# Moving the gathers, four weight loads and the selection's evictions across the overflow branch of two mixture-of-experts layers

## The chip, the cores and the metric

The kernel runs on one core of a Trainium2 chip. The metric is the device time of one execution in microseconds (us); less is better. TensorE (PE in the profile, PEld for its weight loads), VectorE (DVE), ScalarE (ACT), GpSimd (POOL) and SyncE (SP) each run their own instruction stream in order and wait for one another through semaphores. SP and POOL, and now and then ACT, also issue DMA transfers.

## The reference

Two transformer layers over 256 latent and 256 context tokens of width 1024. Each layer has a mixer (Fourier and neighbourhood attention in layer 0, retention in layer 1) and then a mixture of 16 experts, of which each token uses two. Only the experts matter here:

```python
def moe_ffn(tok, router_w, router_b, w1, w3, w2):
    scores = jax.nn.sigmoid((tok @ router_w).astype(jnp.float32))
    ...
    for e in range(N_EXPERTS):
        hid = jax.nn.silu(tok @ w1[e]) * (tok @ w3[e])
        out = out + gate[:, e:e + 1] * (hid @ w2[e])
    return out
```

Layer 0 feeds 512 tokens to the experts, layer 1 the 256 latent ones.

## The kernel before

Every weight matrix of an expert comes as two tiles of 1 MB (`raw`, 128 partitions by 2048 floats), six tiles for an expert: two each of `moe_w1`, `moe_w3` and `moe_w2`. `split` turns a tile into four halves' worth of operands: ScalarE rounds each half to `whi` (L176), VectorE subtracts to get `wlo` (L178), and TensorE makes three products for every weight block (`mm3`, L317 to L319): `whi` with `xh`, `wlo` with `xh`, `whi` with `xl`. `raw` tiles rotate through six slots, `whi`/`wlo` pairs through a small ring of their own, so loads wait until a slot has been split and splits until a pair has been multiplied.

The rows of one expert are brought together first. In **layer 0** (`moe`, `expert`) the router gives each expert up to 128 tokens, in a list `tok`. `e_gather(e)` (L1018) is an indirect DMA on GpSimd's queue that fetches expert e's rows of `xd` into `xg[e % 2]`; `e_tr(e)` transposes them on TensorE (`tsp`, L670) and splits them into `xh`, `xl`. The hidden value `g` (L1064, L1065) is transposed (`tsp`, L670) and split into `gh`, `gl` and multiplied by `moe_w2` into `y_ps`. In **layer 1** (`moe1`, `expert1`) the router gives each group of four experts up to 128 tokens. Group 0's rows are not gathered: `select_group0` multiplies the tokens with a selection matrix on TensorE (`sel_ps`, L1432), and its evictions write `xh` (ScalarE, L1436) and `xl` (VectorE, L1437). Groups 1 to 3 are gathered.

Where more than 128 tokens fall to an expert or a group, extra passes are needed. They stand in a branch over all engines (`overflow`, L1101, and `overflow1`, L1553): every engine loads the flag `R["ovf"]` into a register (L690, L1451) and jumps over the body when it is zero, which is the case in the runs here. `branch_hint` places a prefetch hint on each engine ahead of it. On GpSimd the path around the body waits for the DMAs that GpSimd has issued and then adds to their semaphores what the body would have added (INC_SWDGE_SEM).

The Tile scheduler orders each engine's stream: among what is ready in its own plan it takes what was traced first. So work traced behind the branch can be issued ahead of it, if it doesn't depend on the branch's body. `issue_after(ins)` adds an edge of order alone: what the block traces on the engine of `ins` is queued behind `ins`.

Before the change, layer 0 traces the register load (L690), sets up the experts (`experts_setup`, which also writes zeros into `xg`, L1028), traces the branch, and behind it the gather for expert 0, two tiles of `moe_w3` and two of `moe_w2` of expert 0 loaded from GpSimd's queue (L157 with `self.ld = nc.gpsimd`), the gather for expert 1, the transposes of expert 0, and the gather for expert 2. All other weight tiles are loaded from SP's queue. Layer 1 traces the selection, products and evictions, ahead of its branch, with the products in PSUM bank set `psp`.

Of the kernel before, what the change touches and what calls it, by code (L numbers as in the profile page):

```python
# [7 lines left out]
F32 = mybir.dt.float32  # L8
# [3 lines left out]
AF = mybir.ActivationFunctionType  # L12
ALU = mybir.AluOpType
# [92 lines left out]
def weight_block(A, name, layer, e, k, n):  # L106
    key = ((layer, e), 0, 4, 512 * n, 512) if name == "moe_w2" else ((layer, e), k - k % 4, 4, 0, 512)
    return A[name][TILE_AT[name][key], :, 512 * (k % 4):512 * (k % 4) + 512]


class Net:
# [564 lines left out]
    def moe(self, layer, NT):  # L676
        nc = self.nc
        assert layer == 0
        with ExitStack() as es:
            rp = self.pool(es, f"moe_r{layer}", 1)  # L680
            psp = self.pool(es, f"moe_tp{layer}", 3, space=PSUM)
            hps = self.pool(es, f"moe_h{layer}", 3, space=PSUM)
            yps = self.pool(es, f"moe_y{layer}", 2, space=PSUM)
            fin = [self.ada_mm(1, c, (hps, "h"), psp) for c in self.fill]
            self.prefetch([("moe_w1", (0, 0), 4 * i, 4, 0, 512) for i in range(2)])
            R = self.route(layer, NT, rp, psp)
            with self.tc.issue_after(R["dve"].ins):
                for f in fin:
                    f()
            rv = nc.values_load(R["ovf"][0:1, 0:1], min_val=0, max_val=1)  # L690
            self.branch_hint(layer, R)
            self.g2 = [self.mod_bc(rp, layer, G2, i, tag=f"g2{i}") for i in range(NT // 2)]
            ep = self.pool(es, f"moe_e{layer}", 2)
            self.xs = [[ep.tile([128, 8, 128], F32R, name=f"{n}{i}", bufs=1) for n in ("xh", "xl")] for i in range(2)]
            self.facc = ep.tile([128, 2, D], F32, name="facc", bufs=1)
            last = R["dve"]
            after = lambda: (es2.enter_context(self.tc.issue_after(i.ins)) for i in (last, self.rt_act))
            with ExitStack() as es2:
                list(after())
                xg = self.experts_setup(layer, NT, R, ep, psp, hps, yps)  # L700
            self.overflow(rv, self.facc[:, 0], self.facc[:, 1])
            with ExitStack() as es2:
                list(after())
                es2.enter_context(self.tc.issue_after(self.zeroed.ins))
                first = self.e_gather(0)
                es2.enter_context(self.tc.issue_after(first.ins))
                self.ld = nc.gpsimd
                self.prefetch([("moe_w3", (0, 0), 4 * i, 4, 0, 512) for i in range(2)])
                self.prefetch([("moe_w2", (0, 0), 0, 4, 512 * n, 512) for n in range(2)])
                self.ld = nc.sync  # L710
                self.e_gather(1)
                self.e_tr(0)
                self.e_gather(len(xg))
                self.e_hid(0, "moe_w1", 0)
                R["weights"]()
                self.expert(0)
            for e in range(1, 16):
                self.expert(e)
            self.hx.close()
            self.moe0_tail(ep, psp, hps)  # L720
# [699 lines left out]
        nc.vector.tensor_tensor(gw, gw, tb[:, 16:32], ALU.add)  # L1420
        return nc.vector.tensor_tensor(gw, gw, tb[:, 32:48], ALU.add)

    def select_group0(self, NT, R, P, psp):
        nc = self.nc
        xh, xl = self.xs[0]
        for t in range(NT):
            nc.vector.tensor_scalar(P[:, t], self.cb[:, 2], 1.0, R["rs0"][:, t:t + 1], ALU.add, ALU.is_equal)
        for b0 in (0, 4):
            tp = psp.tile([128, 512], F32, tag="tp", name="sel_ps")
            for b in range(4):  # L1430
                for t in range(NT):
                    nc.tensor.matmul(tp[:, 128 * b:128 * b + 128],  # L1432
                                     self.xm[t][:, 128 * (b0 + b):128 * (b0 + b) + 128], P[:, t],
                                     start=(t == 0), stop=(t == NT - 1))
            tv = tp.rearrange("p (b q) -> p b q", q=128)
            nc.scalar.activation(xh[:, b0:b0 + 4], tv, AF.Copy)  # L1436
            nc.vector.tensor_tensor(xl[:, b0:b0 + 4], tv, xh[:, b0:b0 + 4].bitcast(F32), ALU.subtract)  # L1437

    def moe1(self):
        nc = self.nc  # L1440
        NT = 2
        with ExitStack() as es:
            rp = self.pool(es, "moe_r1", 1)
            psp = self.pool(es, "moe_tp1", 3, space=PSUM)
            hps = self.pool(es, "moe_h1", 3, space=PSUM)
            fin = [self.ada_mm(1, c, (hps, "h"), psp) for c in self.fill]
            R = self.route1(NT, rp, psp)
            with self.tc.issue_after(R["dve"].ins):
                for f in fin:
                    f()  # L1450
            rv = nc.values_load(R["ovf"][0:1, 0:1], min_val=0, max_val=1)  # L1451
            self.branch_hint(1, R)
            self.fg = rp.tile([128, D], F32, name="fng")
            nc.gpsimd.dma_start(self.fg, self.A["final_norm_g"].partition_broadcast(128))
            self.g2 = [self.mod_bc(rp, 1, G2, 0, tag="g20")]
            yps = self.pool(es, "moe_y1", 1, space=PSUM)
            ep = self.pool(es, "moe_e1", 2)
            self.xs = [[ep.tile([128, 8, 128], F32R, name=f"{n}{i}", bufs=1) for n in ("xh", "xl")] for i in range(2)]
            scr = ep.tile([128, 2, D], F32, name="scr", bufs=1)
            hg = [ep.tile([128, D], F32, name=f"hg{i}", bufs=1) for i in range(4)]  # L1460
            last = R["dve"]
            after = lambda: (es2.enter_context(self.tc.issue_after(i.ins)) for i in (last, self.rt_act))
            self.select_group0(NT, R, scr[:, 0, 0:128 * NT].rearrange("p (t s) -> p t s", s=128), psp)
            xg = self.xg
            self.X = X = dict(layer=1, NT=NT, T=128 * NT, R=R, ep=ep, psp=psp, hps=hps, yps=yps, xg=xg, xs=self.xs,
                              hs={}, per=4, hg=hg, ss=ep.tile([128, 4, 2], F32, name="oss", bufs=1))
            with ExitStack() as es2:
                list(after())
                nc.gpsimd.memset(xg[0], 0.0)
            self.overflow1(rv, scr)  # L1470
            with ExitStack() as es2:
                list(after())
                for g in range(1, 4):
                    self.gather(xg[g - 1], self.xd, R["tok"][:, g:g + 1], 256)
                self.e_hid(0, "moe_w1", 0)
                R["weights"]()
                self.expert1(0)
            for g in range(4):
                nc.gpsimd.memset(hg[g], 0.0)
                self.gather(hg[g], self.hd, R["tok"][:, g:g + 1], 256)  # L1480
            for e in range(1, 16):
                self.expert1(e)
            self.hx.close()
# [63 lines left out]
    def overflow1(self, rv, scr):  # L1547
        nc, A, tc, X = self.nc, self.A, self.tc, self.X
        V = nc.vector
        NT, R, ep, psp, xg, hg = (X[k] for k in ("NT", "R", "ep", "psp", "xg", "hg"))  # L1550
        x, ya, gT, hr = xg[0], xg[1], xg[2][:, 0:512].rearrange("p (b q) -> p b q", q=128), hg[0]
        xT = scr[:, 1].rearrange("p (b q) -> p b q", q=128)
        with tc.If(rv > 0, label="ovf1"):  # L1553
# [15 lines left out]
            def product(lhs, nk, w):  # L1569
                ps = psp.tile([128, 512], F32, tag="tp", name="f_ps")  # L1570
                for k in range(nk):
                    nc.gpsimd.dma_start(fw, w(k))
                    nc.tensor.matmul(ps, lhs[:, k], fw, start=(k == 0), stop=(k == nk - 1))
                return ps

            for g in range(4):
# [6 lines left out]
                for e in range(4 * g, 4 * g + 4):  # L1583
                    nc.scalar.activation(fg, product(xT, 8, lambda k: weight_block(A, "moe_w1", 1, e, k, 0)),
                                         AF.Silu)
                    ps = product(xT, 8, lambda k: weight_block(A, "moe_w3", 1, e, k, 0))
                    V.scalar_tensor_tensor(fg, ps, gw[:, e:e + 1], fg, ALU.mult, ALU.mult)
                    transposed(gT, fg, 4)
                    for n in range(2):
                        ns = slice(512 * n, 512 * n + 512)  # L1590
                        ps = product(gT, 4, lambda k: weight_block(A, "moe_w2", 1, e, k, n))
# [6 lines left out]
                V.scalar_tensor_tensor(hr, hr, r, self.fg, ALU.mult, ALU.mult)  # L1598
                self.scatter_out(hr, tok[:, g:g + 1])
            self.slots1(NT, R, 0, psp, tok, tokf)  # L1600

    def dump(self, name, view):
        if name in self.dbg:
            self.nc.sync.dma_start(self.dbg[name], view)
# [49 lines left out]
```

## Time and profile before

| | us |
|---|---|
| three timed runs | 1297.39, 1297.54, 1301.25 |
| median of them | 1297.54 |
| the profiled execution's own time | 1300.92 |
| its span, first to last instruction | 1299.1 |

| engine | busy us, share of the span |
|---|---|
| TensorE matmuls | 1208.8, 93% |
| TensorE weight loads | 945.9, 73% |
| VectorE | 941.4, 72% |
| ScalarE | 752.8, 58% |
| GpSimd | 125.9, 10% |

The mean granted clock of TensorE is 0.973 of full speed (1.00 is 2.4 GHz, 0.50 is 1.2 GHz). The experts of layer 0 stand at 330 to 640 us of the span, those of layer 1 at 983 to 1283 us. In a row of a timeline the columns are start, duration, engine, line, operation, written tile, shapes, count of merged instructions, and in brackets how long the engine sat idle before it and what ended that. A letter q behind an engine marks its sequencer.

### The profile page before, as it was taken

Reading aid. Unit: us, or ns where it says so; the run is one execution under the profiler, and the core shown is the slowest. Engines: PE = TensorE matmul, PEld = TensorE weight load, DVE = VectorE, ACT = ScalarE, POOL = GpSimd, SP = SyncE. Lnnn points to the kernel's source line nnn. Section 1 sums busy time; section 2 is a strip of 40 time slices with the busy share of each in tenths; the row PEclk is TensorE's granted clock in tenths of the full one; section 3 lists DMA queues with packets and bytes.
Section 4 is the critical chain, followed back from the end, with each engine's and each line's share of the span. In section 5 each row is a group of like instructions: output and inputs, shape, how many; then the busy total and the mean of one; then the engine's idle time right before and its main releaser. Section 6 shows DMA issues by size and latency. Waiting matters only on the chain. (4 is left out here: it accounts for less than half of the span.)

```text
span 1299.1 us, 18749 instructions
## 1 busy us (share of the span) xinstructions
PE 1208.8 (93%) x7081; PEld 945.9 (73%) x7081; DVE 941.4 (72%) x1593; ACT 752.8 (58%) x1118; POOL 125.9 (10%) x126
## 2 busy tenths in 40 slices
PE   5999999898599999999989999999997999999994
PEld 3777666576488877777667888898776788777673
DVE  4755666856598888888897554454657899888984
ACT  3754565723397778778554333343434787677762
POOL 1010002200211112111000000000003000000020
PEclk8999999999799999999989999999998999999997
DMA  9766673342799999999883445422749899899980
GB/s 344 259 239 253 250 269 141 124 160 82 311 349 373 358 357 359 362 368 349 305 318 113 149 158 202 153 107 97 289 167 391 339 353 376 317 346 349 327 312 9
DMA packets 60885, 340.60 MB, mean 262 GB/s; under 512 B 10252, under 2 KB 14860, under 8 KB 24144
## 3 DMA queue, kind: packets, MB, share of 16 engines
q1 hardware_dynamic: 46656, 303.07, 61.8%
q0 software_dynamic: 11392, 31.81, 7.5%
q10 hardware_dynamic: 2736, 4.41, 1.0%
q8 instruction: 59, 0.97, 0.3%
q14 instruction: 42, 0.34, 0.1%
HBM read 333.74 MB, written 18.40 MB: 271 GB/s over the span
## 5 line engine op out<-in xcount | busy, mean ns | idle before, releaser
L178 DVE TENSOR_TENSOR wlo<-raw,whi 128x1024 fp32r<-128x1024 f32 x471 | 557.6, 1219 | 115.2 <-ACT whi L176 113.8
L176 ACT ACTIVATE whi<-raw 128x1024 fp32r<-128x1024 f32 x476 | 478.3, 1052 | 95.2 <-PE qk_ps L318 24.7
L318 PE MATMUL h_ps<-wlo,xh 128*128 128x512 f32 x512 | 208.9, 408 | 8.2 <-DVE wlo L178 8.0
L317 PE MATMUL h_ps<-whi,xh 128*128 128x512 f32 x512 | 204.3, 400 | 0.0
L319 PE MATMUL h_ps<-whi,xl 128*128 128x512 f32 x512 | 203.9, 398 | 0.1
L318 PEld LDWEIGHTS h_ps<-wlo,xh 128*128 128x128 f32 x512 | 96.8, 189 | 47.2 <-DVE wlo L178 28.3
L317 PEld LDWEIGHTS h_ps<-whi,xh 128*128 128x128 f32 x512 | 96.9, 189 | 21.7 <-ACT whi L176 0.4
L319 PEld LDWEIGHTS h_ps<-whi,xl 128*128 128x128 f32 x512 | 96.8, 189 | 19.5 <-issue 0.5
L274 PE MATMUL ada_ps<-raw,cT 128*32 128x128 f32 x1536 | 54.6, 279 | 0.6 <-DMA raw<-in_ada_w 0.6
L317 PE MATMUL y<-whi,gh 128*128 128x512 f32 x128 | 51.4, 401 | 0.9 <-ACT gh L673 0.9
L318 PE MATMUL y<-wlo,gh 128*128 128x512 f32 x128 | 51.5, 402 | 0.6 <-DVE wlo L178 0.6
L317 PE MATMUL y_ps<-whi,gh 128*128 128x512 f32 x128 | 51.4, 401 | 0.7 <-ACT gh L673 0.7
L318 PE MATMUL y_ps<-wlo,gh 128*128 128x512 f32 x128 | 51.7, 404 | 0.0
L319 PE MATMUL y<-whi,gl 128*128 128x512 f32 x128 | 51.1, 408 | 0.5 <-DVE gl L674 0.4
L319 PE MATMUL y_ps<-whi,gl 128*128 128x512 f32 x128 | 51.2, 405 | 0.1
L274 PEld LDWEIGHTS ada_ps<-raw,cT 128*32 128x32 f32 x1536 | 42.1, 111 | 12.5 <-issue 8.8
L673 ACT ACTIVATE gh<-tsp 128x512 fp32r<-128x512 f32 x32 | 19.1, 597 | 46.8 <-PE tsp L670 46.7
L673 ACT ACTIVATE xh<-tsp 128x512 fp32r<-128x512 f32 x38 | 22.3, 596 | 31.9 <-PE tsp L670 31.9
L317 PE MATMUL qk_ps<-xhi,whi 128*128 128x512 f32 x96 | 39.4, 411 | 0.0
L1092 POOL DMA_INDIRECT moe_sum<-y,tok x15 | 26.2, 1748 | 133.4 <-ACT y L1087 133.4
L318 PE MATMUL qk_ps<-xlo,whi 128*128 128x512 f32 x96 | 38.8, 404 | 0.0
L1018 POOL DMA_INDIRECT xg<-xd,tok x19 | 25.8, 1356 | 130.8 <-PE tsp L670 109.5
(437 smaller groups left out, 2401.1 us busy)
## 6 DMA issues: line engine op xcount, KB each, us to landing
raw<-in_moe_w SPq DMA_DIRECT2D x188, 1024.0 KB, 7.7
raw<-in_ada_w SPq DMA_DIRECT2D x48, 1024.0 KB, 6.6
raw<-in_ret_w_in SPq DMA_DIRECT2D x24, 1024.0 KB, 6.5
raw<-in_mixab_w_in SPq DMA_DIRECT2D x10, 1024.0 KB, 6.4
raw<-in_ret_w_out SPq DMA_DIRECT2D x8, 1024.0 KB, 4.9
raw<-in_mixab_w_out SPq DMA_DIRECT2D x4, 1024.0 KB, 7.0
raw<-in_moe_w POOLq DMA_DIRECT2D x4, 1024.0 KB, 7.9
bias<-in_rpb ACTq DMA_DIRECT2D x12, 256.0 KB, 5.3
```

The lines of the kernel that those rows point to most:

```text
L176: self.nc.scalar.activation(hi, r, AF.Copy)
L178: eng.tensor_tensor(lo, r, hi.bitcast(F32), ALU.subtract)
L274: mm = nc.tensor.matmul(ps[32 * j:32 * j + 32, 0:128], self.cT[:, kk, :], raw[:, k, 128 * j:128 * j + 128], start=(kk == 0), stop=(kk == 7 ...
L317: mm(out, lh, rh, start=first, stop=False)
L318: mm(out, lh, rl, start=False, stop=False)
L319: self.mm_last = mm(out, ll, rh, start=False, stop=last)
L673: nc.scalar.activation(hi[:, b0:b0 + w], tv, AF.Copy)
L1018: return self.nc.gpsimd.indirect_dma_start(out=x, out_offset=None, in_=xd[:, :], in_offset=bass.IndirectOffsetOnAxis(ap=idx, axis=0), boun ...
L1092: nc.gpsimd.indirect_dma_start(out=self.F[:, :], out_offset=bass.IndirectOffsetOnAxis(ap=R["tok"][:, e:e + 1], axis=0), in_=y, in_offset=N ...
```

## The change

In layer 0 the gather for expert 0, the four weight loads from GpSimd's queue and the gather for expert 1 are traced ahead of the branch, in that order, and the register load is queued behind the second gather on GpSimd. The gather for expert 2 stays behind the branch. In layer 1 the selection is cut in two: the products are traced ahead of the branch, now in the bank set `hps`, and the evictions (`split_group0`) behind it. A write to `xh` and `xl` at the end of the branch's body makes the evictions depend on the branch, so that they can't be issued ahead of it.

```diff
-            rv = nc.values_load(R["ovf"][0:1, 0:1], min_val=0, max_val=1)
             self.branch_hint(layer, R)
...
                 xg = self.experts_setup(layer, NT, R, ep, psp, hps, yps)
+                first = self.e_gather(0)
+            with self.tc.issue_after(first.ins):
+                self.ld = nc.gpsimd
+                self.prefetch([("moe_w3", (0, 0), 4 * i, 4, 0, 512) for i in range(2)])
+                self.prefetch([("moe_w2", (0, 0), 0, 4, 512 * n, 512) for n in range(2)])
+                self.ld = nc.sync
+                second = self.e_gather(1)
+            with self.tc.issue_after(second.ins):
+                rv = nc.values_load(R["ovf"][0:1, 0:1], min_val=0, max_val=1)
             self.overflow(rv, self.facc[:, 0], self.facc[:, 1])
             with ExitStack() as es2:
                 list(after())
                 es2.enter_context(self.tc.issue_after(self.zeroed.ins))
-                first = self.e_gather(0)
-                es2.enter_context(self.tc.issue_after(first.ins))
-                self.ld = nc.gpsimd
-                self.prefetch([("moe_w3", (0, 0), 4 * i, 4, 0, 512) for i in range(2)])
-                self.prefetch([("moe_w2", (0, 0), 0, 4, 512 * n, 512) for n in range(2)])
-                self.ld = nc.sync
-                self.e_gather(1)
                 self.e_tr(0)
                 self.e_gather(len(xg))
...
-    def select_group0(self, NT, R, P, psp):
+    def select_group0(self, NT, R, P, ps):
...
-            tp = psp.tile([128, 512], F32, tag="tp", name="sel_ps")
+            tp = ps.tile([128, 512], F32, tag="h", name="sel_ps")
...
+            tps.append(tp)
+        return tps
+
+    def split_group0(self, tps):
+        nc = self.nc
+        xh, xl = self.xs[0]
+        for i, tp in enumerate(tps):
             tv = tp.rearrange("p (b q) -> p b q", q=128)
-            nc.scalar.activation(xh[:, b0:b0 + 4], tv, AF.Copy)
-            nc.vector.tensor_tensor(xl[:, b0:b0 + 4], tv, xh[:, b0:b0 + 4].bitcast(F32), ALU.subtract)
+            b = slice(4 * i, 4 * i + 4)
+            nc.scalar.activation(xh[:, b], tv, AF.Copy)
+            nc.vector.tensor_tensor(xl[:, b], tv, xh[:, b].bitcast(F32), ALU.subtract)
...
             self.overflow1(rv, scr)
             with ExitStack() as es2:
                 list(after())
+                self.split_group0(tps)
                 for g in range(1, 4):
...
             self.slots1(NT, R, 0, psp, tok, tokf)
+            for w in self.xs[0]:
+                V.memset(w.bitcast(F32)[:, 0:8:4, 0:1], 0.0)
```

## Rows read from the trace of the kernel before

**Rows 1.** Windows in layer 0: length, busy of each engine, PEclk, DMA share, GB/s

```profile
325.00:330.00 5.00, 0.20 (x1) 0.00 (x0) 2.62 (x7) 0.00 (x0) 2.27 (x2) 0.50 0.60 186
...
340.00:345.00 5.00, 4.35 (x19) 3.23 (x18) 2.69 (x5) 3.89 (x4) 0.00 (x0) 1.00 1.02 431
...
350.00:355.00 5.00, 1.72 (x8) 1.75 (x9) 0.00 (x0) 0.60 (x1) 0.00 (x0) 0.50 1.02 417
...
400.00:420.00 20.00, 20.00 (x96) 16.07 (x95) 17.41 (x18) 16.35 (x21) 3.01 (x2) 1.00 0.99 376
```

**Rows 2.** Timeline of TensorE in layer 0, around the gather for expert 1

```profile
353.28 1.94 PE L670 MATMUL tsp<-cst,xg 128*128 128x128 f32 x8 [7.30 <-DMA xg<-xd,tok]
355.01 1.06 PE L670 MATMUL tsp<-cst,g 128*128 128x128 f32 x4
356.46 0.66 PE L670 MATMUL tsp<-cst,xg 128*128 128x128 f32 x2 [0.39 <-DMA xg<-xd,tok]
356.77 0.78 PE L317 MATMUL y_ps<-whi,gh 128*128 128x512 f32 x1
```

**Rows 3.** Timeline of GpSimd's issues in layer 0: gathers and weight loads

```profile
325.02 1.68 POOL L1018 DMA_INDIRECT xg<-xd,tok  x1 [8.39 <-DVE adab L282]
326.70 0.60 POOL L157 DMA_DIRECT2D raw<-in_moe_w  x1
334.99 1.65 POOL L157 DMA_DIRECT2D raw<-in_moe_w  x3 [7.70 <-PE h_ps L319]
336.95 1.41 POOL L1018 DMA_INDIRECT xg<-xd,tok  x1 [0.30 <-issue]
```

**Rows 4.** Line 1101, layer 0's branch: duration ns min/median/max, first and last start

```profile
L1101 POOLq EVENT_SEMAPHORE  x5: 17/43/43, 329.5 to 333.3; - x5
...
L1101 PEldq COMPARE_BRANCH  x1: 3722/3722/3722, 325.4 to 325.4; - x1
...
L1101 DVEq COMPARE_BRANCH  x1: 84/84/84, 325.9 to 325.9; - x1
...
L1101 DVEq EVENT_SEMAPHORE  x1: 21/21/21, 329.3 to 329.3; - x1
L1101 POOLq INC_SWDGE_SEM  x1: 931/931/931, 333.4 to 333.4; - x1
```

**Rows 5.** Issue to landing: the load at 326.70, gathers at 338.67 and 372.68

```profile
DMA to landing us min/median/max: 6.4/6.4/6.4
...
DMA to landing us min/median/max: 17.7/17.7/17.7
...
DMA to landing us min/median/max: 9.8/9.8/9.8
```

**Rows 6.** Timeline of layer 0: VectorE's product g, SP's first loads

```profile
348.48 0.68 DVE L1065 TENSOR_TENSOR g<-g,h_ps 128x512 f32<-128x512 f32 x1
...
337.45 7.21 SPq L157 DMA_DIRECT2D raw<-in_moe_w  x4
```

**Rows 7.** Timeline of layer 1 from the selection to TensorE's longest wait

```profile
971.07 5.77 ACT L176 ACTIVATE whi<-raw 128x1024 fp32r<-128x1024 f32 x6
...
978.70 2.35 DVE L178 TENSOR_TENSOR wlo<-raw,whi 128x1024 fp32r<-128x1024 f32 x2
...
983.51 0.48 PE L317 MATMUL h_ps<-whi,xh 128*128 128x512 f32 x1
...
984.42 0.69 DVE L1437 TENSOR_TENSOR xl<-sel_ps,xh 128x512 fp32r<-128x512 f32 x1 [0.99 <-ACT xh L1436]
...
985.03 4.62 DVE L178 TENSOR_TENSOR wlo<-raw,whi 128x1024 fp32r<-128x1024 f32 x4
...
992.86 0.19 DVE L1375 TENSOR_TENSOR of<-oa,og 128x32 f32<-128x32 f32 x1 [3.21 <-DVEq L1553]
...
1003.15 0.56 PE L318 MATMUL h_ps<-wlo,xh 128*128 128x512 f32 x1 [4.34 <-DVE wlo L178]
```

**Rows 8.** Line 1553, layer 1's branch, on VectorE's sequencer

```profile
L1553 DVEq COMPARE_BRANCH  x1: 74/74/74, 986.9 to 986.9; - x1
```

More of the change, by code (lines that the diff above doesn't have):

```diff
@@ L1421, in slot_weights1 @@
         return nc.vector.tensor_tensor(gw, gw, tb[:, 32:48], ALU.add)
-    def select_group0(self, NT, R, P, psp):
+    def select_group0(self, NT, R, P, ps):
         nc = self.nc
-        xh, xl = self.xs[0]
+        tps = []
         for t in range(NT):
@@ L1462, in moe1 @@
             after = lambda: (es2.enter_context(self.tc.issue_after(i.ins)) for i in (last, self.rt_act))
-            self.select_group0(NT, R, scr[:, 0, 0:128 * NT].rearrange("p (t s) -> p t s", s=128), psp)
+            tps = self.select_group0(NT, R, scr[:, 0, 0:128 * NT].rearrange("p (t s) -> p t s", s=128), hps)
             xg = self.xg
```

## The prediction

> **What bounds the kernel now.** I read the windows first. In the middle of layer 0's experts TensorE is busy for all of a stretch of 20 us, at the full clock of 2.4 GHz [rows 1]; so there the time is TensorE's work, and only what happens ahead of such a stretch can be won or lost, one for one. Next I looked for the holes at the start of each expert stage. The timeline of TensorE in layer 0 has one of 7.30 us, ended by the landing of expert 1's gather, and a small one of 0.39 us for expert 2's gather [rows 2]. Behind the hole the clock stands at 0.50, which is 1.2 GHz, while in the window ahead of it it was 1.00 [rows 1].
>
> Why does that gather land so late? GpSimd issued expert 0's gather at 325.02 and one weight load at 326.70, and then nothing until 334.99 [rows 3]. The releaser printed there is TensorE, but the rows of the branch tell more: GpSimd's sequencer goes through the semaphores of its DMAs until 333.3 and then through the 0.93 us of INC_SWDGE_SEM [rows 4]. The load of 326.70 lands 6.4 us later, at 333.1 [rows 5], just ahead of that. So GpSimd's way around the branch ends only once what GpSimd has issued has landed, and from landing to the next issue it takes 334.99 - 333.1 = 1.9 us. Three loads and the gathers for experts 1 and 2 stand behind it. Meanwhile the DMA engines ran at a share of 0.60 and 186 GB/s; later, with SP's loads added from 337.45 [rows 6], at 431 GB/s, which is full [rows 1]. The gather is late because it was queued late and then had to share.
>
> In layer 1 the hole is on TensorE at 1003.15, 4.34 us, ended by a weight split on VectorE; VectorE itself lost 3.21 us at 992.86 to its own branch [rows 7].
>
> **Layer 0, step by step.** The change takes three loads and expert 1's gather from behind GpSimd's branch and puts them ahead. Issue: three loads take 1.65 us in all [rows 3], so they would go out from 327.3 to 329.0 and the gather at about 329.2, 7.7 us earlier than 336.95. They need `raw` slots that layer 1's two modulation chunks leave; the load at 326.70 took one of the same four slots without a wait.
>
> Landing: the first load should land at 333.1 as before. Each further MB (1.05e6 bytes) takes 1.05/0.431 = 2.4 us at the full rate, three take 7.3 us, and the gather's 0.52e6 bytes 1.2 us: 341.6 with nothing beside them. SP's loads start at 337.45 and share the tail; if the last 2.2 us of work go at half rate it is 343.8. At half rate from the start it would be 333.1 + 17 = 350. I take 344, near the first, because SP's slots still have to be split before it can load.
>
> What is late next: TensorE's last product ahead of the hole ends at 353.28 - 7.30 = 345.98 [rows 2], so a gather at 344 costs nothing. Then comes `g`. VectorE made it at 348.48 (0.68 us) [rows 6], behind splits of a `moe_w2` tile that had only just landed; with that tile landing some 8 us earlier these splits can come first. From the transposes of `g` to the first `y_ps` it takes 356.77 - 355.01 = 1.76 us [rows 2]. So `y_ps` starts between 345.98 + 0.68 + 1.76 = 348.4 and 348.48 + 0.68 + 1.76 = 350.9, against 356.77: 8.3 to 5.9 us are won. More is possible, since the low clock after the hole goes with it (the eight transposes at 353.28 took 1.94 us at 1.2 GHz; at 2.4 GHz half of that is an estimate of 1.0 won). Less is possible, since VectorE's splits all crowd forward. I take -6.5 us, with -9 and -3 as ends.
>
> What waits for the added order: behind GpSimd's branch stands expert 2's gather, and behind that expert 0's scatter, which isn't needed before 360. GpSimd's branch itself costs nothing to others as long as that gather is in time (the rivals). The branch may also come later on the other engines, because the scheduler now has more time to place work ahead of it. TensorE's branch took 3.72 us, 325.4 to 329.1, and VectorE's 3.4 us, 325.9 to 329.3 [rows 4], both under the wait for expert 0's gather (issued at 325.02; at the 6.4 us of the load behind it, it lands about 331). If one of them comes behind the first transposes, that cover is gone and it costs between 0 and 3.7 us; most of that VectorE and TensorE have in hand before 345.98, since they wait for loads. I take 0, inside the ends above. SP and ScalarE leave their branch at once, nothing there.
>
> **Layer 1, step by step.** No work is added; the two evictions on ScalarE and the two on VectorE now stand behind the branch, and every product on `h_ps` needs them. The bank set `hps` has three banks, two of which the modulation chunks hold until VectorE has added their bias, ahead of its split at 978.70, so the products aren't held for long. ScalarE is idle and its branch is short. VectorE decides. It can split only the six halves that ScalarE has rounded (x6 at 971.07); at 4.62/4 = 1.16 us each from 978.70 it is done at 985.6 [rows 7]. Before, its branch was taken at 986.9 [rows 8] with work queued to 985.03 + 4.62 = 989.65, so the sequencer runs 2.7 us ahead; now it would branch at 982.9. From branch to next instruction it was 992.86 - 986.9 = 6.0 us here [rows 7, 8], and 3.4 us in layer 0 [rows 4]. So the first `xl` (0.69 us) is there between 982.9 + 3.4 + 0.7 = 987.0 and 982.9 + 6.0 + 0.7 = 989.6. TensorE starts `h_ps` at 983.51 now [rows 7]; it would start in earnest 3.5 to 6.1 us later. Against that VectorE has no gap at 992.86 any more (3.21 us), and TensorE no hole of 4.34 us at 1003.15 [rows 7], for VectorE does the same splits either way. The two cancel to -0.8 to +1.8 us; the low clock that followed one hole may follow the other. I take 0, with -3.5 and +3 as ends, for VectorE's later small waits may go too.
>
> [...]
>
> **The sum.** -6.5 + 0 = -6.5 us. The profiled execution took 1300.92 us (span 1299.1), so it would take 1294.4; that execution is 3.4 us above the median of the timed runs, 1297.54, and the same difference from the median gives 1291.
>
> **The rivals.** *A, the forecast*: both holes of layer 0 go; 1291 (1287 to 1294). For it: the loads have free slots and idle DMA engines; 0.45.
>
> *B, the hole moves to expert 2's gather.* TensorE takes its stream in order, and that stream has expert 2's transposes right behind those of `g`, ahead of most of `y_ps` [rows 2]. Now that gather can't be issued until all that GpSimd issued has landed: 344 + 1.9 = 345.9. With 6.4 us to landing (the nearest uncontended row) it is there at 352.3, with 9.8 us at 355.7 [rows 5]. If the scheduler leaves those transposes where they are, TensorE waits there instead of at 353.28 and wins only 356.46 - 352.3 = 4.2 to 0.8 us, 2.5 as a middle: 1295. Against it: the scheduler orders by its own plan, and with weights there earlier it has other products to place first; 0.22.
>
> *C, the same place, slower.* The gather for expert 2 took 17.7 us to land when SP's loads filled the engines [rows 5]. If expert 1's gather lands at 348 and this one takes 9.8 to 17.7 us, it is there at 348 + 1.9 + 9.8 = 359.7 to 367.6, and TensorE stands until then: 3 to 11 us worse than 356.46, 1302 with 4.5. It decides from the moment that this landing falls behind 356.46, and only if the transposes keep their place; 0.15. [...]
>
> *D, layer 1 loses.* VectorE's splits ahead of the branch and the fetch add up, and the clock falls in the new hole: +3 us, so 1294 with A's gain; 0.10.
>
> *E, nothing of it shows*: the loads are issued early but `y_ps` waits for VectorE's splits all the same: 1297; 0.08.
>
> **How the numbers follow.** About 0.3% (3.9 us) is what a measurement of this kernel can tell from no change. Faster by more: nearly all of A, a third of B, some of D: 0.43 + 0.07 + 0.04 = 0.54. Slower by more: most of C and a little elsewhere: 0.14. Within: 0.32. For 8 in 10 the range leaves out the best tenth of A, where the clock's gain and layer 1's -3.5 us come together below 1285, and the worse half of C above 1300: 1285 to 1300.
>
> **What would show it.** Right: GpSimd's four loads and two gathers in a row from 325 to 331; expert 1's gather landed by 346; no wait above 1 us at TensorE's second set of transposes; the first `y_ps` near 350 and the clock at 1.00 through 345 to 360. In layer 1: VectorE's wait behind its branch ahead of the first `xl`, TensorE's first `h_ps` at 987 to 990, and no hole near 1003. Wrong: a wait for expert 2's gather at 347 to 360 (B, C), a branch on TensorE or VectorE in the midst of the first products, or a new hole above 6 us behind the selection's products (D).

## The result, and the profile after it

| | before | changed kernel |
|---|---|---|
| median of the timed runs, side by side, us | 1298.60 | 1290.39 |
| lowest and highest of them, us | 1295.5, 1301.74 | 1287.46, 1293.8 |
| ratio, 95% interval | | 0.993 (0.9915 to 0.9946) |
| the profiled execution's own time, us | 1300.92 | 1289.99 |
| its span, us | 1299.1 | 1288.2 |

The change makes the kernel 0.7% faster, 8.2 us between the medians. The forecast was 6.5 us, all of it from layer 0. The size is near; the place is not. Run alone, layer 0's part is worth nothing that can be measured, and layer 1's part is worth 7.4 us.

In the profile after it the line numbers of layer 0 have moved by 1 (L1102 is the branch, L1019 the gather), those of layer 1 by 1 to 10 (L1433 is the selection's product, L1446 the eviction `xl`, L1563 the branch).

**Layer 0.** GpSimd's issues, in a timeline of the changed kernel (start, duration, engine, line, operation, tile, count, idle time before and what ended it), answer to [rows 3]:

```profile
324.61 1.68 POOL L1019 DMA_INDIRECT xg<-xd,tok  x1 [8.40 <-DVE adab L282]
326.30 2.15 POOL L157 DMA_DIRECT2D raw<-in_moe_w  x4
328.75 1.05 POOL L1019 DMA_INDIRECT xg<-xd,tok  x1 [0.30 <-issue]
347.46 1.01 POOL L1019 DMA_INDIRECT xg<-xd,tok  x1 [17.65 <-PE h_ps L319]
```

The issue from gather 1 to its landing, which answers to [rows 5]:

```profile
DMA to landing us min/median/max: 16.8/16.8/16.8
```

Four loads and two gathers go out in a row, and gather 1, issued at 328.75, lands at 345.5. That much is as forecast. Now TensorE's timeline of the same stretch, which answers to [rows 2]:

```profile
336.22 1.94 PE L670 MATMUL tsp<-cst,xg 128*128 128x128 f32 x8 [11.43 <-DVEq L1102]
337.99 0.79 PE L317 MATMUL h_ps<-whi,xh 128*128 128x512 f32 x1
...
348.38 1.03 PE L670 MATMUL tsp<-cst,xg 128*128 128x128 f32 x8
...
353.52 0.50 PE L317 MATMUL h_ps<-whi,xh 128*128 128x512 f32 x1 [1.31 <-ACT xh L673]
...
355.28 0.80 PE L319 MATMUL h_ps<-whi,xl 128*128 128x512 f32 x1 [1.02 <-DVE xl L674]
...
359.86 0.43 PE L317 MATMUL y_ps<-whi,gh 128*128 128x512 f32 x1
```

The transposes of expert 1 (348.38) start without a wait: the hole of 7.30 us is gone. But the first transposes, of expert 0, start at 336.22 behind 11.43 us of idle time, which VectorE's branch ended; before, they started at 330.56 behind 5.36 us, as two lines of the kernel before show that [rows 2] doesn't have:

```profile
330.56 1.94 PE L670 MATMUL tsp<-cst,xg 128*128 128x128 f32 x8 [5.36 <-DMA xg<-xd,tok]
...
343.14 0.50 PE L318 MATMUL h_ps<-wlo,xh 128*128 128x512 f32 x1 [0.65 <-DVE wlo L178]
```

Add up the holes of the stretch: before, 5.36 + 0.65 + 7.30 + 0.39 = 13.70 us; now 11.43 + 1.31 + 1.02 = 13.76 us. The hole moved, and its sum stayed.

Why VectorE's branch is late shows in the timelines of ScalarE (first line) and VectorE, and in the rows of the branch:

```profile
332.46 2.00 ACT L176 ACTIVATE whi<-raw 128x1024 fp32r<-128x1024 f32 x2 [11.01 <-DMA raw<-in_moe_w]
```

```profile
328.81 1.03 DVE L785 TENSOR_SCALAR S<-cb,tokf 128x128 fp32r<-128x128 bf16 x4
333.55 2.36 DVE L178 TENSOR_TENSOR wlo<-raw,whi 128x1024 fp32r<-128x1024 f32 x2 [3.72 <-ACT whi L176]
336.06 0.36 DVE L965 TENSOR_TENSOR t<-of,sc 128x64 f32<-128x64 f32 x2
```

```profile
L1102 DVEq COMPARE_BRANCH  x1: 84/84/84, 335.1 to 335.1; - x1
L1102 DVEq EVENT_SEMAPHORE  x1: 21/21/21, 335.9 to 335.9; - x1
```

Ahead of the branch now stand two splits (333.55) that were not there before. They are those of expert 0's first `moe_w3` tile, the load that GpSimd issues at 326.30 and that lands at 332.4. With that load ahead of the branch, the scheduler had its splits to place ahead of the branch too. VectorE waits 3.72 us for them, takes its branch at 335.1 instead of 325.9 [rows 4], and TensorE's transposes wait for VectorE behind that branch. The way around the branch isn't the cost: from branch to next step it is 0.8 us here, at 335.95, and VectorE was in its split until 335.91.

**Layer 1.** The timelines of TensorE, VectorE and ScalarE and the branch's rows of the changed kernel answer to [rows 7, 8]:

```profile
974.72 3.62 PE L1433 MATMUL sel_ps<-scr,xg 128*128 128x128 f32 x30
983.36 0.80 PE L317 MATMUL h_ps<-whi,xh 128*128 128x512 f32 x1 [5.03 <-issue]
```

```profile
975.65 6.89 DVE L178 TENSOR_TENSOR wlo<-raw,whi 128x1024 fp32r<-128x1024 f32 x6
982.70 0.19 DVE L1376 TENSOR_TENSOR of<-oa,og 128x32 f32<-128x32 f32 x1 [0.16 <-DVEq L1563]
...
983.39 1.28 DVE L1446 TENSOR_TENSOR xl<-sel_ps,xh 128x512 fp32r<-128x512 f32 x2
```

```profile
982.71 1.08 ACT L1445 ACTIVATE xh<-sel_ps 128x512 fp32r<-128x512 f32 x2 [8.42 <-DVEq L1563]
```

```profile
L1563 DVEq COMPARE_BRANCH  x1: 74/74/74, 976.1 to 976.1; - x1
...
L1563 DVEq EVENT_SEMAPHORE  x1: 21/21/21, 982.6 to 982.6; - x1
```

VectorE does its six splits in one go from 975.65 to 982.54. Its sequencer had handed all six to the engine and taken the branch by 976.1, so whatever the branch costs passes under them: 0.16 us of idle time are left of the 3.21 us in [rows 7]. TensorE pays a hole of 5.03 us ahead of the first `h_ps`, and there is no hole behind it up to 1013. The write that ties the evictions to the branch is VectorE's, for `xh` as for `xl`; so ScalarE's `xh` waits 8.42 us for VectorE's branch, and the first `h_ps` with it.

For both layers it helps to count TensorE's products. Each layer's experts make 1152 products of 128x512 (lines 317 to 319), so the start of the n-th says how far the work is. The tables give those starts in us as the trace has them, for layer 0 from the start of gather 0, for layer 1 from the start of the last modulation product (L274); the kernels beside before and after are those of the next section.

| layer 0 | 1st | 37th | 73rd | 289th | 1152nd |
|---|---|---|---|---|---|
| before | 7.3 | 17.1 | 38.6 | 93.0 | 316.7 |
| changed kernel | 13.4 | 24.6 | 37.9 | 92.3 | 313.7 |
| layer 0 alone | 13.6 | 24.7 | 37.9 | 92.3 | 313.8 |
| splits deferred | 8.5 | 29.8 | 39.8 | 94.2 | 315.7 |
| deferred, gather 1 first | 7.6 | 23.1 | 34.5 | 88.9 | 310.8 |
| deferred, gather 1 in the middle | 7.3 | 18.5 | 34.3 | 88.7 | 310.2 |
| gather 1 in the middle, not deferred | 13.2 | 24.0 | 38.8 | 93.2 | 314.7 |

| layer 1 | 1st | 37th | 73rd | 145th | 1152nd |
|---|---|---|---|---|---|
| before | 10.1 | 18.9 | 34.1 | 53.4 | 309.4 |
| layer 0 alone | 7.2 | 16.1 | 31.9 | 51.3 | 307.9 |
| evictions free again | 7.2 | 16.1 | 32.0 | 51.3 | 305.8 |
| changed kernel | 12.5 | 22.5 | 31.4 | 48.6 | 301.0 |
| layer 1 alone | 12.8 | 22.8 | 31.7 | 48.8 | 301.3 |
| splits behind the branch | 11.1 | 23.9 | 34.4 | 52.1 | 305.9 |

### The profile page after: what moved, and what is told of

Read it like the earlier page. It is cut to its first block, busy times and chain, and to the rows that moved or that the text cites. A ratio compares the mean times of both kernels' runs of the same rounds, so it can differ in the third digit from the quotient of the medians.

```text
span 1288.2 us, 18793 instructions
## 1 busy us (share of the span) xinstructions
PE 1197.9 (93%) x7081; PEld 943.8 (73%) x7081; DVE 943.1 (73%) x1593; ACT 755.2 (59%) x1118; POOL 126.1 (10%) x126
## 5 line engine op out<-in xcount | busy, mean ns | idle before, releaser
L274 PE MATMUL ada_ps<-raw,cT 128*32 128x128 f32 x1536 | 53.6, 275 | 1.6 <-DMA raw<-in_ada_w 1.5
L317 PE MATMUL y_ps<-whi,gh 128*128 128x512 f32 x128 | 51.3, 401 | 0.7 <-ACT gh L673 0.7
L274 PEld LDWEIGHTS ada_ps<-raw,cT 128*32 128x32 f32 x1536 | 41.3, 109 | 13.2 <-issue 8.7
L318 PE MATMUL qk_ps<-xlo,whi 128*128 128x512 f32 x96 | 38.8, 404 | 0.0
L319 PE MATMUL qk_ps<-xhi,wlo 128*128 128x512 f32 x96 | 38.4, 400 | 0.0
L1554 POOL DMA_INDIRECT out_dram<-hg,tok x4 | 11.0, 2740 | 260.2 <-DVE hg L1548 209.4
```

The lines of the kernel that those rows point to most:

```text
L274: mm = nc.tensor.matmul(ps[32 * j:32 * j + 32, 0:128], self.cT[:, kk, :], raw[:, k, 128 * j:128 * j + 128], start=(kk == 0), stop=(kk == 7 ...
L317: mm(out, lh, rh, start=first, stop=False)
L318: mm(out, lh, rl, start=False, stop=False)
L319: self.mm_last = mm(out, ll, rh, start=False, stop=last)
L1554: self.nc.gpsimd.indirect_dma_start(out=self.out[:, :], out_offset=bass.IndirectOffsetOnAxis(ap=idx, axis=0), in_=x, in_offset=None, bound ...
```

## The experiments

Theory 1 is the prediction: the gain is layer 0's, -6.5 us, and layer 1 gives nothing. Theory 2 is read from the trace above: layer 0's hole only moved, and layer 1 gains because VectorE's branch lies under work that is already queued.

**One layer at a time.** The first kernel has the diff in `moe` alone, the second the rest of it (`select_group0`, `split_group0`, `moe1`, `overflow1`).

> Layer 0's part of the change, with layer 1 as before. Theory 1 (the prediction): expert 1's gather lands by 346, its hole of 7.30 us goes, the whole gain is here: -6.5 us, a ratio of 0.995 (0.993 to 0.998). Theory 2 (read from the trace of the changed kernel): the hole only moves. TensorE's first transposes start at 336.2 instead of 330.6, since VectorE's branch now stands behind the split of a moe_w3 tile that lands at 332.4; so what is won at 353 is lost at 330, layer 0 is worth 0 to -3 us, a ratio of 0.998 to 1.000.

Measured: ratio 0.9997 (0.9985 to 1.0009), that is -0.4 us (-2.0 to +1.2).

> Layer 1's part of the change, with layer 0 as before. Theory 1 (the prediction): 0 us (-3.5 to +3), a ratio of 0.997 to 1.002. Theory 2 (from the trace of the changed kernel): VectorE now takes its branch at the start of its six splits, not behind them, so the code fetch passes under work that is queued already, and TensorE's hole near 1003 goes; layer 1 is worth -5 to -8 us, a ratio of 0.994 to 0.996.

Measured: 0.9943 (0.9924 to 0.9962), -7.4 us (-9.9 to -4.9). By the intervals theory 2 fits both, theory 1 neither. No trace shows what VectorE's branch waits for, a fetch of code or anything else. The trace of layer 0 alone has the same holes as the changed kernel:

```profile
336.93 1.94 PE L670 MATMUL tsp<-cst,xg 128*128 128x128 f32 x8 [11.62 <-DVEq L1102]
...
354.04 0.50 PE L317 MATMUL h_ps<-whi,xh 128*128 128x512 f32 x1 [1.17 <-ACT xh L673]
...
355.79 0.80 PE L319 MATMUL h_ps<-whi,xl 128*128 128x512 f32 x1 [1.02 <-DVE xl L674]
```

**Is it the `moe_w3` split that holds the branch?** In this kernel ScalarE and VectorE may not take the splits of expert 0's `moe_w3` before they have evicted its transposes, which stand behind the branch. `transpose_split` returns its last two instructions, and:

```diff
-                self.e_tr(0)
+                self.tr0 = self.e_tr(0)
...
-        self.e_hid(e, "moe_w3", 0)
+        with ExitStack() as q:
+            for i in self.tr0 if e == 0 else ():
+                q.enter_context(self.tc.issue_after(i.ins))
+            self.e_hid(e, "moe_w3", 0)
```

> The changed kernel, with the splits of expert 0's moe_w3 tiles queued behind the evictions of its transposes on ScalarE and VectorE, so that they cannot stand ahead of the branch there. Theory 2: the first transposes start at 330 to 333 instead of 336.2, and TensorE then meets expert 1's gather (landing at 345.5) or the moe_w3 splits earlier than it has them: of the 3.2 to 6.2 us some 3 remain, 3 us below the changed kernel, a ratio to the kernel before of 0.990 to 0.992. Rival: the landing of the moe_w3 tiles binds anyway, and the two kernels are the same, 0.993.

Measured: 0.9924 (0.9904 to 0.9945). TensorE's timeline, and gather 1's landing, in this kernel:

```profile
333.55 1.94 PE L670 MATMUL tsp<-cst,xg 128*128 128x128 f32 x8 [6.54 <-DVE wk L971]
...
355.01 1.94 PE L670 MATMUL tsp<-cst,xg 128*128 128x128 f32 x8 [9.29 <-DMA xg<-xd,tok]
```

```profile
DMA to landing us min/median/max: 23.9/23.9/23.9
```

The step itself is shown: VectorE's branch is taken at 328.4, and the first transposes start 333.55 - 326.83 = 6.7 us behind gather 0's issue instead of 11.6. Gather 0 lands at 333.4 in this kernel, so next to nothing of that start is VectorE's any more. But the time isn't measurably below the changed kernel's; it lies as near to the rival's 0.993 as to theory 2's range, for a reason that neither named. The hole at gather 1 is back, and longer than before the change: 9.29 us. Gather 1 was issued at 330.97 and needed 23.9 us. The cause is on SP's queue, in its timelines of the changed kernel (first line) and of this one (second):

```profile
335.94 1.41 SPq L157 DMA_DIRECT2D raw<-in_moe_w  x3
```

```profile
328.86 13.37 SPq L157 DMA_DIRECT2D raw<-in_moe_w  x3
```

SP's loads for expert 1 wait for slots too. In the changed kernel SP's first load waits until the `moe_w3` tile has landed (332.46) and then for VectorE, and starts at 335.94, between the end of that tile's second split (335.91) and VectorE's first step behind the branch (335.95); two more loads stand behind it. So what held SP back were the same splits that made the branch late. With them deferred SP's first load starts at 328.86, right behind an older split that ends at 328.83, the loads share the DMA engines with GpSimd's queue (share 0.99 to 1.01 in the windows from 330 to 355), and gather 1, the last in that queue, comes at 354.9. So the two terms that the prediction took one by one, the landing at 344 and the branch at no cost, could not both be had with this order of GpSimd's queue.

**The order of the bytes.** With the splits deferred, gather 1 is put straight behind gather 0, or between the `moe_w3` and the `moe_w2` tiles:

```diff
             with self.tc.issue_after(first.ins):
+                second = self.e_gather(1)
+            with self.tc.issue_after(second.ins):
                 self.ld = nc.gpsimd
```

> As the run with the deferred splits, and expert 1's gather issued straight behind expert 0's, ahead of the four weight loads. If that gather's landing is what comes next, it lands near 334 instead of 345.5, and the time falls by up to 3 us more: a ratio of 0.988 to 0.990. If the moe_w3 tiles come next, which now go out 1.5 us later, it is 0 to 1.5 us slower than that run.

Measured: 0.990 (0.988 to 0.9919).

> The run with the deferred splits, with the order of GpSimd's queue gather 0, two moe_w3 tiles, gather 1, two moe_w2 tiles. If what bounds the start of layer 0 is which bytes come first, this order has both the moe_w3 tiles and gather 1 by 343, the waits for moe_w3 (1.38 and 0.77 us in the run with gather 1 first) go, and it is 1 to 2 us below that run: a ratio to the kernel before of 0.988 to 0.990. If SP's loads for expert 1 share the engines with it, gather 1 lands at 347 or later and it is as slow as the changed kernel: 0.992 to 0.993.

Measured: 0.9904 (0.9887 to 0.9921), a median of 1287.13 us beside 1299.34 of before and 1290.06 of the changed kernel, which ran once more beside it:

> The changed kernel once more, unaltered, so that the others of this call have it beside them: a ratio of 0.992 to 0.995.

Measured: 0.9935 (0.9916 to 0.9955). TensorE's waits at the start of layer 0 with gather 1 in the middle are:

```profile
329.38 1.94 PE L670 MATMUL tsp<-cst,xg 128*128 128x128 f32 x8 [5.33 <-DVEq L1109]
...
348.72 0.79 PE L317 MATMUL h_ps<-whi,xh 128*128 128x512 f32 x1 [3.25 <-ACT xh L673]
...
350.28 0.80 PE L319 MATMUL h_ps<-whi,xl 128*128 128x512 f32 x1 [0.34 <-DVE xl L674]
```

These are 5.33 + 3.25 + 0.34 = 8.92 us of holes instead of 13.76, and the 289th product starts at 88.7 instead of 92.3. Both orders beat both kernels by their medians. The intervals of the two orders overlap, so the middle order, expected to be 1 to 2 us the faster one, isn't shown to be so. Those of the changed kernel overlap them a little, so for the 3 us between them the trace (3.5 us in layer 0) is a second witness.

The middle order without the deferred splits tells which of the two parts does it:

> The changed kernel with gather 1 between the moe_w3 and the moe_w2 tiles, and the moe_w3 splits left free to go ahead of the branch. Theory 2: those splits still hold VectorE's branch until the moe_w3 tile has landed, the first transposes start 11 to 12 us behind gather 0's issue as in the changed kernel, and the earlier gather finds nobody who waits for it: the changed kernel's time, a ratio of 0.992 to 0.995. Rival (the order of the bytes alone is what helps): 0.989 to 0.991, as with the splits deferred.

Measured: 0.9935 (0.9914 to 0.9956), the changed kernel's time. The two kernels with gather 1 in the middle also show what SP's loads do to it: its landing takes 8.6 us where SP's first load starts at 334.36 (not deferred) and 14.4 us where it starts at 325.90 (deferred). An earlier gather alone finds nobody who waits for it, as long as VectorE's branch is late; an early branch alone finds the gather late. It takes both.

One step more: the `moe_w2` splits of expert 0 queued behind the evictions of expert 1's transposes, to take away the 3.25 us.

> Deferred moe_w3 splits, gather 1 between the tiles, and besides the moe_w2 splits of expert 0 queued behind the evictions of expert 1's transposes on ScalarE and VectorE. In the run with gather 1 between the tiles TensorE waited 3.25 us for ScalarE's xh of expert 1, which stood behind two moe_w2 halves. If that wait is the next one, it goes and the time falls by 1 to 3 us: a ratio to the kernel before of 0.988 to 0.990. If the moe_w2 splits are then late for y_ps, nothing is won: 0.990 to 0.992.

Measured: 0.9951 (0.9929 to 0.9972), worse than without that step, and outside both ranges that were named for it. The 3.25 us went down to 0.71, but other waits came up behind it:

```profile
345.80 0.50 PE L317 MATMUL h_ps<-whi,xh 128*128 128x512 f32 x1 [0.71 <-ACT xh L673]
...
350.64 0.66 PE L670 MATMUL tsp<-cst,g 128*128 128x128 f32 x4 [1.56 <-DVE g L1073]
...
357.50 1.30 PE L670 MATMUL tsp<-cst,xg 128*128 128x128 f32 x5 [3.18 <-DMA xg<-xd,tok]
```

The last one is expert 2's gather, and with it the prediction's rivals B and C: GpSimd can issue that gather only when all its loads have landed (INC_SWDGE_SEM from 349.6, the gather at 351.47, landed 5.9 us later). In the changed kernel it went out at 347.46 and nobody waited for it.

**What layer 1's gain is.** First, is it the order or the bank set? Layer 1's part alone, without the write in the branch's body that ties the evictions to the branch:

```diff
-            for w in self.xs[0]:
-                V.memset(w.bitcast(F32)[:, 0:8:4, 0:1], 0.0)
```

> Layer 1's part alone without the write to xh and xl in the branch's body, so that the evictions may go ahead of the branch again; each engine's stream is then that of the kernel before, and only the bank set of the products differs. Theory 2: the gain comes from the order, so there is none: a ratio of 0.999 to 1.001. Rival: the bank set (psp is left free for other work) is worth a part of it: 0.996 to 0.998.

Measured: 0.9997 (0.9981 to 1.0012). The scheduler put the evictions ahead of the branch again, and with that the whole gain was gone and TensorE's hole of 4.3 us was back. The bank set is worth nothing; the order is all of it.

Second, is it that the branch is covered (theory 2a), or that no split stands in line behind an eviction (2b)? Layer 1's part alone, with VectorE's splits queued behind the branch and behind `xl`, so that nothing covers the branch (`split_group0` returns its last instruction):

```diff
-                self.split_group0(tps)
+                es2.enter_context(self.tc.issue_after(self.split_group0(tps).ins))
```

> [...] Theory 2a (the gain is the covered fetch): VectorE idles 5 to 6.5 us ahead of the first xl, its six splits (7 us) end that much later, the hole on TensorE comes back, and most of the 7.4 us that layer 1's part was worth is lost: a ratio to the kernel before of 0.998 to 1.001. Theory 2b (the gain is that no split waits in line behind an eviction that waits for the selection): TensorE needs a new split every 2.8 us and VectorE makes one in 1.2 us, so only 0 to 1.5 us are lost: 0.9945 to 0.996.

Measured: 0.9998 (0.9987 to 1.0009). All of the 7.4 us is lost. The timelines of TensorE, ScalarE and VectorE and VectorE's branch in this kernel:

```profile
977.12 5.24 PE L1432 MATMUL sel_ps<-scr,xg 128*128 128x128 f32 x30
```

```profile
983.69 1.09 ACT L1444 ACTIVATE xh<-sel_ps 128x512 fp32r<-128x512 f32 x2 [7.02 <-DVEq L1563]
```

```profile
977.64 0.49 DVE L282 TENSOR_TENSOR adab<-ada_ps,adab 128x128 f32<-128x128 f32 x2
984.32 1.29 DVE L1445 TENSOR_TENSOR xl<-sel_ps,xh 128x512 fp32r<-128x512 f32 x2 [6.19 <-ACT xh L1444]
```

```profile
L1563 DVEq COMPARE_BRANCH  x1: 74/74/74, 978.1 to 978.1; - x1
...
L1563 DVEq EVENT_SEMAPHORE  x1: 21/21/21, 983.6 to 983.6; - x1
```

With no work queued the way around the branch takes 983.6 - 978.1 = 5.5 us, ScalarE's `xh` waits for it, and VectorE stands 6.19 us. The six splits, 6.9 us of work, start 12.3 us behind the last modulation product, where in layer 1 alone they are over by 12.0; TensorE's 73rd product comes at 34.4 instead of 31.7. So the gain hangs on having the splits ahead of the branch. But this run doesn't part the two theories: its splits also stand in line behind both `xl`, and the selection that these need ends at 977.12 + 5.24 = 982.36, only 1.2 us ahead of the branch's end.

VectorE's timeline of the kernel with the evictions free again parts them:

```profile
981.24 0.68 DVE L1445 TENSOR_TENSOR xl<-sel_ps,xh 128x512 fp32r<-128x512 f32 x1
...
982.98 0.68 DVE L1445 TENSOR_TENSOR xl<-sel_ps,xh 128x512 fp32r<-128x512 f32 x1
983.58 4.62 DVE L178 TENSOR_TENSOR wlo<-raw,whi 128x1024 fp32r<-128x1024 f32 x4
990.73 0.19 DVE L1375 TENSOR_TENSOR of<-oa,og 128x32 f32<-128x32 f32 x1 [2.53 <-DVEq L1562]
```

Here the first product comes at 7.2 in the table, as with layer 0 alone, and not at 10.1. Both `xl` find their input ready and no split waits behind them, so what 2b names doesn't occur. From its first split at 978.98 up to 1002 the only wait that VectorE's timeline names are the 2.53 us at the branch. TensorE's hole of 4.32 us is there all the same, and the 145th product comes at 51.3 instead of 48.8, 2.5 us later. That is what 2a says, though no kernel without the branch was run. In the kernel before as profiled, where the selection ran at the lower clock (granted 0.61 from 975 to 980), VectorE also waited 0.56 and 0.99 us at the two `xl`; that much of its difference belongs to 2b.

## Why the prediction was right, and where it was not

The total came out as forecast, 1291 against 1290.39, and two wrong terms made it: layer 0 was put at -6.5 us and measured -0.4, layer 1 at 0 and measured -7.4.

*What bounds the kernel.* Right: behind the start of each expert stage TensorE is busy nearly all the time (20.00 us from 400 to 420 in both profiles, 18.5 to 20.0 us of every 20 from 1060 to 1260 in the kernel before), and what was won ahead of it in layer 1 reached the end. The profiles give the clock as a share, not in GHz. In the kernel before, products of 512 columns start 0.427 us apart at 0.50 (1003.51 to 1006.07) and 0.233 us apart at 1.00 (404.62 to 407.42); the 1.2 GHz is an estimate from the first, at a column per cycle, and the 2.4 GHz twice that, as the shares are. Eight transposes took 1.94 us at 0.50 [rows 2] and 1.03 us at 1.00 (348.38 in the changed kernel).

*Layer 0, issue and landing.* Right: gather 1 went out at 328.75 (forecast 329.2) and landed at 345.5 (344, between 341.6 and 350). But it landed there because SP was held back until 335.94, by the very splits that made VectorE's branch late and cost TensorE its start. With SP free at 328.86 it landed at 354.9, outside the bounds. The half rate behind the 350 was an estimate; measured were 23.9 us to landing with SP's loads beside it from the start and 16.8 us with SP held back. The step that SP's slots "still have to be split before it can load" was right about the slots and blind to what else ordered them.

*Layer 0, the branch on the other engines.* This is the step that failed. The text saw that the scheduler might place more ahead of the branch, priced that by the branch's own duration (0 to 3.7 us), and took 0. What moved ahead was a split that waits for a DMA, so the price was that landing: the first transposes start 336.22 - 324.61 = 11.6 us behind gather 0's issue instead of 330.56 - 325.02 = 5.5, which is 6.1 us. The cover named for it (TensorE and VectorE have time in hand before 345.98) was no cover: the products that follow the transposes filled that time. One of the prediction's own rows already told it: the load at 326.70 lands 6.4 us later [rows 5], and whatever splits that tile can't be done before 333.

*Layer 0, the first `y_ps` near 350.* Wrong: 359.86, against 356.77 before. It follows from the step above, though TensorE had done 61 products of `h_ps` by then instead of 48. By the 73rd product the changed kernel is 0.7 us ahead of the kernel before, in the table.

*Layer 1, the start.* The first product was to come 3.5 to 6.1 us later. It comes 12.5 - 10.1 = 2.4 us later than in the kernel before as profiled, which is less than the bounds, and 5.3 us later than in the two traces where it came at 7.2 (layer 0 alone, evictions free again). The size was about right; the reasons weren't, for the bounds hold a gap on VectorE that didn't come, and leave out that ScalarE's eviction waits for VectorE's branch.

*Layer 1, VectorE's branch.* Mis-sized. The text let the sequencer run 2.7 us ahead, as [rows 7, 8] have it, and so left a gap of 3.4 to 6.0 us. That 2.7 us was a count of what happened to be queued behind one wait, not a limit. With six splits whose inputs are ready the sequencer is 982.54 - 976.14 = 6.4 us ahead, and the gap is 0.16 us. Whether more than six can be queued over the branch was not shown.

*Layer 1, what comes back.* Mis-sized. The 3.21 and 4.34 us were to cancel the later start. From the 37th to the 73rd and on to the 109th product TensorE takes 15.2 + 10.4 us in the kernel before and 8.9 + 8.3 in the changed one, 8.4 us less: the hole of 4.34 us and, behind it, products 0.43 us apart instead of 0.23 at the lower clock (a granted clock of 0.55 from 1003.2 to 1007). The changed kernel pays the lower clock too (0.50 from 984 to 986.5), behind its hole of 5.03 us, but only 1.2 us of it (10.0 instead of 8.8 us for the first 36 products). By the 145th product it is 4.8 us ahead. Another 2.3 us come from the products 397 to 649 (63.4 us before, 61.1 now); the timeline names waits of only 0.28 and 0.31 us there, so most of it is in gaps too short to be named. The text had such waits only as an end of its range. The rest of the 8.4 us at the last product, 1.4 us, comes behind the 649th and isn't the new order's: the stretch takes 132.0 us in the kernel before and 130.6 in the changed one, but 131.9 in the second trace of the changed one.

*The length of VectorE's branch.* The prediction let it take 3.4 to 6.0 us in layer 1, and rival D, like the expectations for layer 1, speaks of a fetch there. No run shows such a fetch as what the branch waits for. What they show is its length: 5.5 us in the run with the splits behind the branch, near the longer end, and 0.16 us of VectorE's time when six splits are queued over it. In layer 0 it took 3.4 us in the kernel before, with the DMA engines at a share of 0.60 (325 to 330), and at most 0.8 us in the changed kernel, with them full (share 1.00 in the windows from 330 to 340), so full DMA engines alone didn't make it long.

*The rivals.* A has the number and not the reason. B and C did not come in the changed kernel; the last experiment on layer 0 shows their mechanism at 3.18 us. D had the wrong sign. E, that nothing of layer 0 shows, is what layer 0 did, by another way than E's.

## What to carry to other kernels

When a load is moved ahead of a barrier, follow what consumes it, on every engine: the scheduler may move the consumer ahead too, and then the barrier waits for the landing (VectorE's branch at 335.1 instead of 325.9). A branch cost its engine next to nothing here (0.16 us) where ready work was queued over it, so put it right behind a block of instructions whose inputs are there, and not behind one that waits. And where a stage starts from full DMA queues, as layer 0 does here (share 1.00 from 330 to 340), work that is late on one engine may be what keeps another queue back (SP's first load at 335.94 instead of 328.86); undoing one wait alone can bring an older one back (9.29 us at gather 1), so the order of the bytes and the waits have to be changed together.

## What the runs showed of the hardware

- An indirect gather of 0.5 MB took from 4.1 us to land (gather 2 with the splits deferred, issued when all else of GpSimd's queue had landed) to 23.9 us (gather 1 of the same kernel, behind four loads of 1 MB and beside SP's).
- VectorE's way around a branch that is taken, from the branch to its next step, took 3.4 us in layer 0 of the kernel before and at most 0.8 us in the changed one; in layer 1 it took 5.5 us with the splits behind the branch and 5.8 us in the kernel before, where VectorE's prefetch hint had been issued 8.7 us ahead of the branch (978.20 to 986.9). It was at most 0.8 us in all four traces in which layer 0's hint came 11.3 to 11.7 us ahead of the branch (323.61 to 335.1 in the changed kernel), and 3.4 us where it came 1.9 us ahead (324.02 to 325.9 in the kernel before). What decides this was not tried.
- In the kernel before, the selection's 30 products took 6.14 us, in the changed kernel 3.62 us, with nearly the same work ahead of them. The windows in which they lie (length, busy of each engine, PEclk, DMA share, GB/s), first of before, then of the changed kernel, have the granted clock:

```profile
975.00:980.00 5.00, 3.35 (x20) 3.19 (x20) 4.05 (x22) 1.84 (x2) 1.53 (x2) 0.61 1.01 380
```

```profile
972.00:977.00 5.00, 3.06 (x29) 2.87 (x29) 4.46 (x25) 2.29 (x3) 2.02 (x3) 1.00 0.98 375
```

  What decides between the two was not tried. With layer 1 as before, 2.9 us of the start hang on it by the author's estimate (10.1 or 7.2 to the first product); with its new order none, since TensorE waits for VectorE anyway (12.8 with a slow selection in layer 1 alone, 12.5 with a fast one in the changed kernel). So up to 2.9 us of the difference between the two profiles of layer 1 may be chance; the verdict of the timed runs doesn't rest on it.
- Layer 0's profiles show 3 us that no timing confirms. From gather 0 to the 1152nd product the four traces with the old layer 0 take 315.9 to 317.2 us, the three with the changed one 313.2 to 313.8; 2 us or more of it lie behind the 289th product. Yet the timed runs of layer 0 alone give -0.4 us (-2.0 to +1.2). In its one trace layer 1, unchanged there, has a wait of 1.66 us at 1056.96 that the kernel before and the kernel with the evictions free again don't have; one execution can't tell whether that belongs to the change. Where the 3 us go stays open.
